# Where operands begin in a 512-byte line: other places for weights and for the low parts of inputs

## The chip, the cores and the metric

The kernel runs on one core of a Trainium2 chip. Its time is the device time in microseconds (us). Three runs of the kernel before gave 2886.08, 2892.32 and 2893.58 us; the median is 2892.32 us. The execution that the profile shows took 2885.26 us.

## The reference

Two networks of two layers each run one after the other on 256 tokens of width 1024 in 32-bit floats; the output of the first is the input of the second. The first network has a gated delta rule, a sliding-window attention and a squared-ReLU MLP; the second has two streams ("h", the tokens, and "c", a context of 256 tokens), attention, a short convolution and SwiGLU MLPs:

```
proj = rmsnorm(x, pre_mix_g) @ w_in                    # 1024 -> 7440
y_a = deltanet_branch(...) @ w_up_dn;  y_b = swa_sink_branch(...) @ w_up_sw
x = x + rmsnorm((sigmoid(gate_a) * y_a + sigmoid(gate_b) * y_b) @ w_o, post_mix_g)
x = x + rmsnorm(square(relu(rmsnorm(x, pre_mlp_g) @ w_ff1)) @ w_ff2, post_mlp_g)
# second network, twice per layer for each stream, around context_mix / latent_mix:
swiglu(u, wi, wo) = (silu(g) * up) @ wo,  with g, up = split(u @ wi)      # 1024 -> 2 x 2816 -> 1024
```

Nearly all arithmetic is in the products with the weights `w_in`, `w_ff1`, `w_ff2`, `ffn_wi`, `ffn_wo` and the output projections.

## The kernel before

**Products in three parts.** Every weight and every input of these products is kept as a high part and a low part, both of type fp32r (4 bytes). One product of 128 rows is three matmuls, in `mm3` (L264, L265, L266): high by high, high by low, low by high. In each, `lhsT` is the stationary operand (128 columns, loaded into the array by a weight load, "PEld") and `rhs` is the moving operand, read column by column.

**Two forms.** `lin_b` makes the weights stationary: tiles of 256 columns, called narrow here, of which each product takes 128; the moving operand is then 256 tokens of the input (`xTh`, `xTc`, `oT`). `lin_a`, `out_mm` and the first products of `layer1` make the inputs stationary (128 tokens) and let the weights move: tiles of 512, 432 or 384 columns, called wide. `by_tokens` is an exception: the tile is narrow, and its weights are the moving operand, 256 columns at a time, with the inputs stationary.

**The stages of a weight tile.** `wtile` (L231) issues a DMA of raw weights on SyncE's queue, ScalarE copies it to the high part (`hi`, L210) and VectorE subtracts for the low part (`lo`, L198). `hi` and `lo` have three buffers each.

**Places in a line.** A line here is 512 bytes (128 floats) of one partition's memory. All pools are padded (tiles tagged "line") so that tiles begin at a multiple of 512 bytes. `shifted` (L185) allocates each weight tile with 128 floats to spare and lets it begin further on: wide tiles at 0, narrow `hi` tiles at float 48 (byte 192), narrow `lo` tiles at float 96 (byte 384):

```
by = 0 if n > 256 else 48 if tag[:2] == "hi" else 96
flat = self.t(pool, [P, kt * n + 128], tag, F32R, bufs=bufs)
return flat[:, by:by + kt * n].rearrange("p (k n) -> p k n", n=n)
```

The inputs (`xTh`, `xTc`, made by `Norm.run`, L148), the MLPs' hidden rows (`hid`), `oT` and `mT` begin at byte 0, high and low parts alike. In a tile of 512, 384 or 256 columns every row of the tile is a multiple of 512 bytes long, so each begins at the place of its tile. A row of 432 columns is 1728 bytes, three lines and 192 bytes: four rows that follow each other begin at bytes 0, 192, 384 and 64.

**What sets the order.** The program's order is fixed when the kernel is built, by a scheduler that knows data dependences and priorities. `heads_by_columns` (L1277) prepares the queries of the second network's attention: `qs` and `qz` tiles of three buffers each; GpSimd clears `qz` (L1289) before ScalarE fills it.

Of the kernel before, what the change touches and what calls it, by code (L numbers as in the profile page):

```python
# [9 lines left out]
F32R = mybir.dt.float32r  # L10
# [7 lines left out]
P = 128  # L18
D = 1024
S = 256  # L20
KB = D // P
# [121 lines left out]
class Norm:  # L143


    def __init__(self, k, f, names=("h",)):
        self.k, self.f, self.names, self.x = k, f, names, {}

    def run(self, st, tb):
        if st.name not in self.names:  # L150
            return
        if st.name not in self.x:
            k = self.k
            self.x[st.name] = [k.t(k.xpool if st.name == "h" else k.xpool2, [P, KB, S], "xT" + st.name, F32R, bufs=2) for _ in range(2)]
        back = self.f(st, tb, *self.x[st.name])
        self.k.deferred.append([DEFER * 800, (st.name, tb), back])

# [6 lines left out]
class Kern:  # L164
    def __init__(self, tc, I, out, dbg=None):
        self.tc, self.nc, self.I, self.out, self.dbg = tc, tc.nc, I, out, dbg
        self.uid = 0
        self.flip = self.nraw = 0
        self.deferred = []
        self.credit = self.ada_rate = 0.0  # L170

# [13 lines left out]
    def shifted(self, pool, kt, n, tag, bufs):  # L185


        by = 0 if n > 256 else 48 if tag[:2] == "hi" else 96
        flat = self.t(pool, [P, kt * n + 128], tag, F32R, bufs=bufs)
        return flat[:, by:by + kt * n].rearrange("p (k n) -> p k n", n=n)  # L190

# [1086 lines left out]
    def heads_by_columns(self, ap, st, pj, qk, tb, kT):  # L1278


        nc = self.nc
        kh, kl, kb = kT
        qf = qk.rearrange("p h d -> p (h d)")
        s = slice(tb * P, (tb + 1) * P)
        q = None
        if st.full:
            q = self.t(ap, [P, 6, P], "qs", F32R, bufs=3), self.t(ap, [P, 2, 3, P], "qz", bufs=3)
            for d in range(2):
                nc.gpsimd.memset(q[1][64 - 64 * d:128 - 64 * d, d], 0.0)  # L1289
            for b in range(2):  # L1290
                ps = self.psum([P, 3, P])
                for j in range(3):
                    src = qf[:, j * P:(j + 1) * P] if b == 0 else pj[:, 384 + j * P:384 + (j + 1) * P]
                    nc.tensor.transpose(ps[:, j, :], src, self.ident)
                if b == 0:
                    self.stack_q(q[0], ps, 0.125)
                else:
                    for d in range(2):
                        r = slice(64 * d, 64 * d + 64)
                        self.act(q[1][r, d], ps[r], scale=0.125)  # L1300
        kd = self.t(self.work, [P, 4, 64], "w2", bufs=3)
        for d in range(2):
            nc.vector.tensor_copy(kd[:, d::2, :], qk[:, 6:8, :])
        kdf = kd.rearrange("p a d -> p (a d)")
        for j0, m in ((0, 2), (2, 3)):
            ps = self.psum([P, 3, P])
            for j in range(m):
                src = kdf[:, j * P:(j + 1) * P] if j0 == 0 else pj[:, 1024 + j * P:1024 + (j + 1) * P]
                nc.tensor.transpose(ps[:, j, :], src, self.ident)
            if j0 == 0:  # L1310
                self.split_psum(kh[:, :, s], kl[:, :, s], ps[:, :m, :])
            else:
                nc.vector.tensor_copy(kb[:, :, s], ps[:, :m, :])
        return q
# [193 lines left out]
```

## Time and profile before

| | |
|---|---|
| median of the three runs | 2892.32 us |
| the profiled execution | 2885.26 us |
| its span (first to last instruction) | 2883.5 us |
| TensorE busy | 2804.2 us (97%) |
| weight loads busy | 2608.6 us (90%) |
| VectorE busy | 2131.3 us (74%) |
| ScalarE busy | 1333.5 us (46%) |
| mean granted TensorE clock | 0.994 |

A matmul's record is longer than the time until the next one starts, since matmuls are pipelined: a record of 256 columns takes some 0.28 us, while the next one starts 0.12 us later. So the pace is read from the starts, as start of the last row minus start of the first, over the number of matmuls between them. Below, a triple is the three matmuls of one `mm3`.

### The profile page before, as it was taken

How to read it: one execution, taken by the hardware profiler on the slowest of the kernel's cores; microseconds unless marked ns; L12 is line 12 of the kernel's file. 1: busy time of each engine (PE TensorE's matmuls, PEld its weight loads, DVE VectorE, ACT ScalarE, POOL GpSimd, SP SyncE). 2: the span in 40 equal slices, each digit the busy share in tenths (PEclk: the TensorE clock that was granted, in tenths of full speed). 3: DMA queues.
4: the chain of work that ended last, by engine and by line, in shares of the span. 5: the costliest groups of instructions: out<-in, count | busy, mean ns of one | idle time of the engine just before them, and what ended most of it. 6: DMA issues, size and time to landing. Idle time of an engine off the chain costs nothing.

```text
span 2883.5 us, 51232 instructions
## 1 busy us (share of the span) xinstructions
PE 2804.2 (97%) x19840; PEld 2608.6 (90%) x19840; DVE 2131.3 (74%) x5043; ACT 1333.5 (46%) x2627; POOL 5.2 (0%) x16
## 2 busy tenths in 40 slices
PE   8999999999999999999999999999999999999998
PEld 7999988889989888999988988998989999888897
DVE  8888667897876778778698788877686554666764
ACT  6555454565545655332243556332353323446543
POOL 0000000000000000000000000000000000000000
PEclk9999999999999999999999999999999999999999
DMA  6632457655225566455435243555444442341564
GB/s 223 181 103 74 147 180 236 199 172 168 81 75 181 187 216 193 129 158 164 125 114 180 69 132 88 162 154 154 140 132 142 143 125 89 100 133 42 159 192 140
DMA packets 443908, 416.76 MB, mean 145 GB/s; under 512 B 18320, under 2 KB 383760, under 8 KB 443664
## 3 DMA queue, kind: packets, MB, share of 16 engines
q1 hardware_dynamic: 443664, 413.49, 47.2%
q8 instruction: 156, 2.56, 0.4%
q14 instruction: 88, 0.72, 0.1%
HBM read 412.37 MB, written 1.05 MB: 143 GB/s over the span
## 4 chain that ended last, share of the span: by engine, by line
PE 82%; DVE 9%; DMA 4%; ACT 4%; issue 2%; SPq 0%; DVEq 0%; ACTq 0%
PE mm L265 22%; PE mm L264 22%; PE mm L266 22%; PE sm L563 2%; DVE lo L198 2%; PE sm L515 2%; DVE acc L201 2%; PE sm L552 1%; DMA araw<-in_w_ada 1%; PE sm L805 1%; PE sm L800 1%; ACT hi L210 1%; PE sm L264 1%; PE sm L265 1%; PE sm L266 1%
## 5 line engine op out<-in xcount | busy, mean ns | idle before, releaser
L198 DVE TENSOR_TENSOR lo<-raw,hi 128x1024 fp32r<-128x1024 f32 (+2 forms) x628 | 750.4, 1206 | 334.6 <-ACT hi L210 333.5
L210 ACT ACTIVATE hi<-raw 128x1024 fp32r<-128x1024 f32 (+2 forms) x628 | 647.5, 1046 | 735.7 <-PE mm L265 314.0
L264 PE MATMUL mm<-xTh,hi 128*128 128x256 f32 x2336 | 655.7, 281 | 3.0 <-ACT xTh L210 3.0
L265 PE MATMUL mm<-xTh,hi 128*128 128x256 f32 x2336 | 652.7, 279 | 0.8 <-DVE xTh L201 0.8
L266 PE MATMUL mm<-xTh,lo 128*128 128x256 f32 x2336 | 649.2, 278 | 0.0
L265 PEld LDWEIGHTS mm<-xTh,hi 128*128 128x128 f32 x2336 | 442.2, 189 | 1.5 <-DVE xTh L201 1.2
L264 PEld LDWEIGHTS mm<-xTh,hi 128*128 128x128 f32 x2336 | 438.1, 188 | 3.7 <-ACT xTh L210 3.5
L266 PEld LDWEIGHTS mm<-xTh,lo 128*128 128x128 f32 x2336 | 438.4, 188 | 0.1
L201 DVE SCALAR_TENSOR_TENSOR acc<-araw,csil,acc 128x256 f32<-128x256 f32 x896 | 390.6, 479 | 64.3 <-DMA araw<-in_w_ada 61.6
L264 PE MATMUL mm<-hi,hid 128*128 128x512 f32 x872 | 340.4, 390 | 0.0
L266 PE MATMUL mm<-hi,hid 128*128 128x512 f32 x872 | 339.6, 389 | 0.0
L265 PE MATMUL mm<-lo,hid 128*128 128x512 f32 x872 | 339.5, 389 | 0.0
L264 PE MATMUL mm<-xTc,hi 128*128 128x256 f32 x1104 | 309.3, 280 | 0.0
L265 PE MATMUL mm<-xTc,hi 128*128 128x256 f32 x1104 | 307.1, 278 | 0.0
L266 PE MATMUL mm<-xTc,lo 128*128 128x256 f32 x1104 | 305.7, 277 | 0.0
L265 PEld LDWEIGHTS mm<-xTc,hi 128*128 128x128 f32 x1104 | 208.6, 189 | 0.4
L264 PEld LDWEIGHTS mm<-xTc,hi 128*128 128x128 f32 x1104 | 206.6, 187 | 0.4
L266 PEld LDWEIGHTS mm<-xTc,lo 128*128 128x128 f32 x1104 | 206.5, 187 | 0.1
L266 PEld LDWEIGHTS mm<-hi,hid 128*128 128x128 f32 x872 | 163.7, 188 | 34.2
L265 PEld LDWEIGHTS mm<-lo,hid 128*128 128x128 f32 x872 | 163.7, 188 | 33.4 <-DVE lo L198 0.2
L264 PEld LDWEIGHTS mm<-hi,hid 128*128 128x128 f32 x872 | 163.7, 188 | 33.1
L264 PE MATMUL mm<-hi,xTh 128*128 128x256 f32 (+3 forms) x512 | 178.0, 349 | 4.8 <-ACT xTh L1157 3.6
(323 smaller groups left out, 4647.8 us busy)
## 6 DMA issues: line engine op xcount, KB each, us to landing
raw<-in_ffn_wi SPq DMA_DIRECT2D x352, 256.0 KB, 3.7
araw<-in_w_ada SPq DMA_DIRECT2D x288, 256.0 KB, 2.9
raw<-in_w_ff SPq DMA_DIRECT2D x128, 512.0 KB, 4.1
raw<-in_w_in SPq DMA_DIRECT2D x116, 512.0 KB, 3.8
raw<-in_ffn_wo SPq DMA_DIRECT2D x88, 512.0 KB, 4.0
raw<-in_w_o SPq DMA_DIRECT2D x40, 512.0 KB, 3.4
raw<-in_w_in SPq DMA_DIRECT2D x24, 432.0 KB, 4.9
raw<-in_w_up_sw SPq DMA_DIRECT2D x16, 512.0 KB, 3.9
```

What stands on the lines that cost most here:

```text
L198: self.nc.vector.tensor_tensor(out=out, in0=a, in1=b, op=op)
L201: self.nc.vector.scalar_tensor_tensor(out=out, in0=a, scalar=s, in1=b, op0=op0, op1=op1)
L210: self.nc.scalar.activation(out, a, func, **kw)
L264: mm(ps, lhsT=ah, rhs=bh, start=first, stop=False)
L265: mm(ps, lhsT=ah, rhs=bl, start=False, stop=False)
L266: mm(ps, lhsT=al, rhs=bh, start=False, stop=last)
L515: nc.tensor.matmul(ps[:, h, o:o + n], lhsT=q, rhs=k, start=m == 0, stop=m == len(qk) - 1)
L552: nc.tensor.transpose(ps[:, b, :], sc[:, b // nb, (b % nb) * P:(b % nb + 1) * P], self.ident)
L563: nc.tensor.matmul(po[:, h, :], lhsT=pT[:, h * nb + kb, :], rhs=v, start=kb == 0, stop=kb == nb - 1)
L800: nc.tensor.matmul(ps[:, i, :], lhsT=LT[:, i, :], rhs=Dm[:, i, :], start=True, stop=True)
L805: nc.tensor.matmul(ps[:, i, :], lhsT=DT[:, i, :], rhs=M[:, i, :], start=True, stop=True)
```

## The change

Three things change, none of them a computation.

- Wide weight tiles begin at one of eight places (0, 64, ... 448 bytes) for `hi`, which goes on by one with every wide tile, and at one of eight for `lo`, which goes on by one with every eighth. Narrow tiles begin at byte 320 (`hi`) and 448 (`lo`).
- The inputs of `Norm` get 128 floats to spare. The high part begins at byte 0 still, the low part at one of the eight places, which goes on by one with every pair of tiles.
- `qz` has two buffers, not three.

```
-            self.x[st.name] = [k.t(..., [P, KB, S], "xT" + st.name, F32R, bufs=2) for _ in range(2)]
+            k.nx += 1
+            flat = [k.t(..., [P, KB * S + 128], "xT" + st.name, F32R, bufs=2) for _ in range(2)]
+            self.x[st.name] = [a[:, by:by + KB * S].rearrange("p (k t) -> p k t", t=S)
+                               for a, by in zip(flat, (0, 16 * (k.nx % 8)))]
...
-        by = 0 if n > 256 else 48 if tag[:2] == "hi" else 96
+        self.nw += n > 256 and tag[:2] == "hi"
+        by = (80 if tag[:2] == "hi" else 112) if n <= 256 else \
+             16 * (self.nw % 8 if tag[:2] == "hi" else self.nw // 8 % 8)
...
-            q = self.t(ap, [P, 6, P], "qs", F32R, bufs=3), self.t(ap, [P, 2, 3, P], "qz", bufs=3)
+            q = self.t(ap, [P, 6, P], "qs", F32R, bufs=3), self.t(ap, [P, 2, 3, P], "qz", bufs=2)
```

No instruction moves: on TensorE (17,550 rows), VectorE, ScalarE and SyncE the two programs have the same operations on the same tiles in the same order. Only waits differ, and most of these are around `qz`. GpSimd's part of the second network's attentions, before (the four `qz` tiles of the first layer, 17847 to 18368; a name in brackets is the engine that is waited for):

```order
L1289 MEMSET qz_17847 64x384 [waits DVE_49,PE_49]
L1289 MEMSET qz_17847 64x384
L1289 MEMSET qz_17903 64x384 x2
L1289 MEMSET qz_18306 64x384 [waits Activation_49]
L1289 MEMSET qz_18306 64x384
L1289 MEMSET qz_18368 64x384 [waits PE_49,Activation_49,Pool_49]
L1289 MEMSET qz_18368 64x384
```

and after:

```order
L1293 MEMSET qz_17847 64x384 [waits DVE_49,PE_49]
L1293 MEMSET qz_17847 64x384
L1293 MEMSET qz_17903 64x384 [waits PE_49]
L1293 MEMSET qz_17903 64x384
L1293 MEMSET qz_18306 64x384 [waits PE_49,Activation_49,Pool_49]
L1293 MEMSET qz_18306 64x384
L1293 MEMSET qz_18368 64x384 [waits PE_49,Activation_49,Pool_49]
L1293 MEMSET qz_18368 64x384
```

The third tile, 18306, now waits for the matmuls that read the first, and the fourth, 18368, for those that read the second.

## Rows read from the trace of the kernel before

**Rows 1.** The page, section 1: TensorE's busy time, share, instructions.

```profile
PE 2804.2 (97%) x19840; PEld 2608.6 (90%) x19840; DVE 2131.3 (74%) x5043; ACT 1333.5 (46%) x2627; POOL 5.2 (0%) x16
```

**Rows 2.** The page, section 4: the chain that ended last.

```profile
PE 82%; DVE 9%; DMA 4%; ACT 4%; issue 2%; SPq 0%; DVEq 0%; ACTq 0%
PE mm L265 22%; PE mm L264 22%; PE mm L266 22%; PE sm L563 2%; DVE lo L198 2%; PE sm L515 2%; DVE acc L201 2%; PE sm L552 1%; DMA araw<-in_w_ada 1%; PE sm L805 1%; PE sm L800 1%; ACT hi L210 1%; PE sm L264 1%; PE sm L265 1%; PE sm L266 1%
```

**Rows 3.** Groups by form: out<-in, shapes, count | busy us, mean ns | idle.

```profile
L264 PE MATMUL mm<-xTh,hi 128*128 128x256 f32 x2336 | 655.7, 281 | 3.0 <-ACT xTh L210 3.0
L265 PE MATMUL mm<-xTh,hi 128*128 128x256 f32 x2336 | 652.7, 279 | 0.8 <-DVE xTh L201 0.8
L266 PE MATMUL mm<-xTh,lo 128*128 128x256 f32 x2336 | 649.2, 278 | 0.0
...
L264 PE MATMUL mm<-hi,hid 128*128 128x512 f32 x872 | 340.4, 390 | 0.0
```

**Rows 4.** Timeline of TensorE, narrow products: start us, length us, instruction.

```profile
1257.67 0.36 PE L264 MATMUL mm<-xTh,hi 128*128 128x256 f32 x1
...
1329.75 0.27 PE L266 MATMUL mm<-xTh,lo 128*128 128x256 f32 x1
...
1400.38 0.28 PE L264 MATMUL mm<-xTc,hi 128*128 128x256 f32 x1
1400.50 0.28 PE L265 MATMUL mm<-xTc,hi 128*128 128x256 f32 x1
1400.62 0.28 PE L266 MATMUL mm<-xTc,lo 128*128 128x256 f32 x1
1400.73 0.28 PE L264 MATMUL mm<-xTc,hi 128*128 128x256 f32 x1
```

**Rows 5.** The same view, wide products of 512 columns (211 matmuls later).

```profile
2815.24 0.40 PE L264 MATMUL mm<-hi,hid 128*128 128x512 f32 x1
...
2863.07 0.48 PE L265 MATMUL mm<-lo,hid 128*128 128x512 f32 x1
```

**Rows 6.** The same view, wide products of 384 columns (95 matmuls later).

```profile
2560.67 0.33 PE L264 MATMUL mm<-hi,xTh 128*128 128x384 f32 x1
...
2577.16 0.34 PE L266 MATMUL mm<-hi,xTh 128*128 128x384 f32 x1
```

**Rows 7.** The same view, wide products of 432 columns (36 matmuls later).

```profile
35.72 0.36 PE L264 MATMUL mm<-hi,xTh 128*128 128x432 f32 x1
...
42.74 0.36 PE L264 MATMUL mm<-hi,xTh 128*128 128x432 f32 x1
```

**Rows 8.** The same view, products by tokens (27 matmuls later).

```profile
2693.15 0.28 PE L264 MATMUL mm<-hi,xTh 128*128 128x256 f32 x1
...
2696.36 0.28 PE L264 MATMUL mm<-hi,xTh 128*128 128x256 f32 x1
```

**Rows 9.** Timeline of TensorE; windows: stretch us, PE busy (count), PEclk, DMA share, GB/s.

```profile
667.61 0.41 PE L264 MATMUL mm<-oT,hi 128*128 128x256 f32 x1
...
669.32 0.33 PE L266 MATMUL mm<-oT,lo 128*128 128x256 f32 x1
...
667.50:669.40 1.90, 1.90 (x11) 0.50 0.02 6
1257.70:1329.70 72.00, 72.00 (x625) 1.00 0.46 140
```

**Rows 10.** Timelines of GpSimd, TensorE and ScalarE: the tiles `qz`.

```profile
1508.53 2.75 POOL L1289 MEMSET qz<- 64x384 f32 x6 [1508.08 <-PE mm L266]
1617.10 0.88 POOL L1289 MEMSET qz<- 64x384 f32 x2 [105.83 <-ACT sc L210]
...
1631.15 1.08 PE L515 MATMUL sm<-kb,qz 128*128 128x256 f32 x4
...
1638.42 0.98 ACT L210 ACTIVATE qz<-sm 64x384 f32<-64x384 f32 x2
1645.18 0.98 ACT L210 ACTIVATE qz<-sm 64x384 f32<-64x384 f32 x2
```

More of the change, by code (lines that the diff above doesn't have):

```diff
@@ L153, in run @@
             k = self.k
-            self.x[st.name] = [k.t(k.xpool if st.name == "h" else k.xpool2, [P, KB, S], "xT" + st.name, F32R, bufs=2) for _ in range(2)]
+            k.nx += 1
+            flat = [k.t(k.xpool if st.name == "h" else k.xpool2, [P, KB * S + 128], "xT" + st.name, F32R, bufs=2) for _ in range(2)]
+            self.x[st.name] = [a[:, by:by + KB * S].rearrange("p (k t) -> p k t", t=S) for a, by in zip(flat, (0, 16 * (k.nx % 8)))]
         back = self.f(st, tb, *self.x[st.name])
@@ L167, in __init__ @@
         self.uid = 0
-        self.flip = self.nraw = 0
+        self.flip = self.nraw = self.nw = self.nx = 0
         self.deferred = []
@@ L185, in shifted @@
     def shifted(self, pool, kt, n, tag, bufs):
-        by = 0 if n > 256 else 48 if tag[:2] == "hi" else 96
+        self.nw += n > 256 and tag[:2] == "hi"
+        by = (80 if tag[:2] == "hi" else 112) if n <= 256 else 16 * (self.nw % 8 if tag[:2] == "hi" else self.nw // 8 % 8)
         flat = self.t(pool, [P, kt * n + 128], tag, F32R, bufs=bufs)
```

## The prediction, made before the changed kernel had run

> **What bounds the kernel now.** I read the page from the top. TensorE is busy for 2804.2 of 2883.5 us [rows 1], and the chain that ended last lies on it for 82%: 22% on each line of `mm3` in tiles `mm` and 1% on each in tiles `sm`, together 69% or 1990 us [rows 2]. No instruction moves, so what is left to read is the pace of these products, and that is in the starts on the timeline, not in the lengths.
>
> Narrow products: 623 starts from 1257.67 to 1329.75 us are 115.7 ns apart in the mean [rows 4]. At a granted clock of 1.00 [rows 9], which is 2.4 GHz, 256 columns at one a cycle are 106.7 ns; each product takes 9.0 ns more. The three lines differ though they have one shape: L264 to L265 and L265 to L266 0.12 us, L266 to the next L264 0.11 us [rows 4], and mean records of 281, 279 and 278 ns [rows 3]. A triple is 347 ns, and with about 117 ns for each of the two longer steps some 113 ns are left for the short one. Wide products: 211 starts in 47.83 us are 226.7 ns apart [rows 5], 13.4 ns over the 213.3 ns of 512 columns; 384 columns take 173.6 ns [rows 6], 13.6 ns over 160.0.
>
> That surcharge is what the change can touch. It belongs to the full clock: at a granted 0.50 (1.2 GHz) 8 starts in 1.71 us are 213.8 ns apart, and 256 columns at 1.2 GHz are 213.3 [rows 9].
>
> **Counts.** Narrow stationary weights: 3,824 triples in four forms (2,336 of them `mm<-xTh,hi`). Wide: 1,224 triples of 512 columns in four forms (872 with `hid`) [rows 3], 96 of 384, 96 of 432. By tokens: 192. (The counts that no row shows are those of the loops.) The paces give 1327 + 833 + 50 + 56 + 68 = 2334 us for all of them; 1990 us of that are on the chain, so I let 0.85 of any change of pace through to the end. The rest would be taken up by waits for VectorE and DMAs that the products now hide.
>
> **Wide weights.** Before, the moving weights and the stationary inputs both begin at byte 0. Other places of moving weights are seen in one form only: rows of 432 columns begin at 0, 192, 384 and 64 in turn. Their pace is 7.02 us for 36, or 195.0 ns [rows 7], 15.0 ns over 180.0. So with places spread over the line the surcharge is 15.0 and not 13.4 to 13.6: 1.5 ns more. The change spreads the wide tiles evenly too: 3 x (1,224 + 96) = 3,960 matmuls x 1.5 ns = 5.9 us. The forms of 432 columns and by tokens stay as they are to me. Bounds: by tokens, where narrow weights move from bytes 192 and 384 over inputs at 0, 27 starts in 3.21 us are 118.9 ns apart [rows 8], a surcharge of 12.2, so 1.2 ns less than at 0 and -4.8 us; if the rows of 432 that begin at 0 have a surcharge of 13.4, the other three have (4 x 15.0 - 13.4) / 3 = 15.5, and were every wide tile off byte 0, that would be 2.1 ns or +8.3 us. I take the middle figure since it is the nearest row: a wide moving operand over an input at 0.
>
> **Low parts of the inputs.** In narrow products they move in L265, one matmul of three; 3,568 of these use tiles of `Norm` (the other 256 have `oT` or the delta rule's output). They too are spread over the line now. At the wide weights' +1.5 ns that is 5.4 us; at the 3.2 ns between by tokens and narrow [rows 4, 8] it would be 11.4 us; the lower end is 0. I take 5.4. In wide products they are the stationary operand of L266 in a quarter of the cases, for which I take 0.
>
> **Narrow weights.** They leave 192 and 384 for 320 and 448. Both are places off byte 0 before and after, and no row shows either new one, so I take 0. Bounds: all three lines at the shortest step, 113 ns, give 339 for 347, -8 ns x 3,824 = -31 us; all three at by tokens' 118.9 give 356.7, +9.7 x 3,824 = +37 us. These two ends are the two rivals with most weight.
>
> **`qz` with two buffers.** The third tile's two clears ran in the row of six at 1508.53 us and now wait as the fourth's do at 1617.10; the first tile's last reader is done by then. ScalarE fills the third tile at 1638.42, 21 us later. The fourth waits for the second tile's last reader, which starts at 1631.15 and is done by 1632.3; the fill is at 1645.18, 13 us later [rows 10]. Behind these clears GpSimd has nothing else. Cost 0; were the cover gone, two pairs of clears of 0.88 us each.
>
> **Sum.** 5.9 + 5.4 = 11.3 us of TensorE's time, x 0.85 = 9.6 us. The profiled execution took 2885.3 us (1.8 us of them around the span), which would become 2894.9. The median of the runs lies 7.1 us above that execution; I predict the median, 2892.3 + 9.6 = 2902 us.
>
> **Rivals.**
>
> *The new pair is the better one (faster).* For it: the short step after L266 shows that one and the same form can go at 113 ns, and L264 and L266 have the same moving operand, so that the weights' places, not the inputs', make the difference. Against: nothing says that 320 and 448 bring it to all three. Price: -31 + 5.9 = -25 us, x 0.85 = -21: 2871 us.
>
> *The distance counts (slower still).* If what decides is how far ahead in the line the weights begin, then the pair before had 192 (L264, L266's next) and 384, and the new one has 320 and 448 less the low part's place. By tokens the inputs are stationary at 0 and the weights move from 192: a distance of -192, which in a line of 512 is 320, and from 384, which is 128 [rows 8]. So L264 and L266 would take the pace of rows 8, and L265 passes all distances. Against it: rows 8 also differ by what moves. Price: (37 + 5.9) x 0.85 = +36: 2929 us. It decides from a narrow triple of 352 ns on, half way.
>
> *Places don't matter (no change).* The surcharge would belong to the fp32r stream as such, 9 ns with 256 columns and 13 to 15 with more. Against it stand the three lines of one shape with steps of 0.11 and 0.12 us [rows 4], and the 3.2 ns between rows 4 and rows 8, which have one shape too. Price: 0, 2892 us. This is where the Trainium skill would put it: "TensorE: Matmul & The Clock Gate", section "Step-by-step: what each phase is for", gives TensorE two independent read ports, one for the streaming operand and one for the weight load, and "SBUF — State Buffer", section "Specifications (TRN2)", has lines of 16 bytes, of which every place here is a multiple. By that rule nothing changes; the trace speaks against it, as the steps of rows 4 show.
>
> **Chances.** Forecast 0.31 (its own range 2893 to 2911), the better pair 0.28, the distance 0.24, no change 0.17. A measurement of this kernel can tell about 0.3%, 8.7 us, from no change. Of the forecast's cases about three in five lie over that, the rest within: slower 0.19 + 0.23 = 0.42. Same: 0.12 + 0.16 and 0.01 from each of the two outer cases = 0.30. Faster: 0.27 and 0.01 of the no-change case = 0.28. The range of 8 in 10 goes out to both outer rivals and a little beyond, 2866 to 2932 us, as the unknown places were bounded from -31 to +37 us.
>
> **What would show it.** In the changed kernel's timeline the narrow triple stays near 347 ns at `xTh` with a low part at byte 0 and gains some 1.5 ns elsewhere; 339 is the first rival, 356 the second. Wide products go from 226.7 to about 228 ns in the mean, with steps that differ from tile to tile as `hi` and `lo` change places; if all stay at 226.7 and the narrow ones at 115.7, places don't matter. The clears of the third and fourth `qz` come near 1617 and 1632 us with no idle time on ScalarE for them. I am wrong if the narrow products' pace moves by more than 2 ns either way, since that alone is worth 20 us.

## The result and the profile after

The changed kernel takes 2923.44 us (median of 4 runs, 2921.45 to 2925.73) against 2891.15 us (4 runs) of the kernel before on the same chip: a ratio of 1.0114, 95% interval 1.0097 to 1.0132. The forecast was 2902 us. The sign is right; the loss of 32 us is more than three times the 9.6 us predicted. The time lies in the stated range, 2866 to 2932 us, and outside the forecast's own, 2893 to 2911.

The profiled span grew by 36.8 us, from 2883.5 to 2920.3 us. The page of the kernel after, section 1 (busy us, share of the span, instructions) and section 4 (chain that ended last, by engine, then by line), in the form of [rows 1, 2]; `mm3` is now L268, L269 and L270:

```profile
PE 2845.8 (97%) x19840; PEld 2638.3 (90%) x19840; DVE 2132.4 (73%) x5043; ACT 1333.8 (46%) x2627; POOL 5.2 (0%) x16
...
PE 83%; DVE 8%; DMA 4%; ACT 3%; issue 1%; SPq 0%; DVEq 0%; ACTq 0%
PE mm L269 22%; PE mm L268 22%; PE mm L270 22%; PE sm L567 2%; DVE lo L202 2%; PE sm L519 2%; PE sm L556 1%; PE sm L809 1%; DVE acc L205 1%; DMA araw<-in_w_ada 1%; PE sm L804 1%; ACT hi L214 1%; PE sm L269 1%; PE sm L268 1%; PE sm L270 1%
```

TensorE is busy for 41.6 us more with the same 19,840 matmuls; VectorE and ScalarE stand where they stood, within 1.1 us. So the span did not grow by new waits: the same products go slower. The groups by form (count | busy us, mean ns of a record | idle), against [rows 3]:

```profile
L269 PE MATMUL mm<-xTh,hi 128*128 128x256 f32 x2336 | 663.9, 284 | 0.8 <-DVE xTh L205 0.8
L268 PE MATMUL mm<-xTh,hi 128*128 128x256 f32 x2336 | 658.8, 282 | 3.0 <-ACT xTh L214 3.0
L270 PE MATMUL mm<-xTh,lo 128*128 128x256 f32 x2336 | 660.7, 283 | 0.0
...
L268 PE MATMUL mm<-hi,hid 128*128 128x512 f32 x872 | 343.8, 394 | 0.0
```

The narrow records were 281, 279 and 278 ns long. It is not only the line that reads the low part (now L269, +5 ns) that got longer: L268 (+1) and L270 (+5) did too, though their moving operand still begins at byte 0. Wide records with `hid` went from 390 to 394 ns.

A group's mean hides that the pace changes from stage to stage. Three stretches of narrow products in the timeline of TensorE in the kernel after (start us, length us, instruction), the first and the last start of each; the low part of the input begins at byte 256, then 128, then 448:

```profile
2195.81 0.28 PE L268 MATMUL mm<-xTh,hi 128*128 128x256 f32 x1
...
2217.24 0.28 PE L268 MATMUL mm<-xTh,hi 128*128 128x256 f32 x1
```

```profile
480.29 0.28 PE L268 MATMUL sm<-xTh,hi 128*128 128x256 f32 x1
...
526.33 0.28 PE L268 MATMUL sm<-xTh,hi 128*128 128x256 f32 x1
```

```profile
2749.35 0.28 PE L268 MATMUL mm<-xTh,hi 128*128 128x256 f32 x1
2749.47 0.29 PE L269 MATMUL mm<-xTh,hi 128*128 128x256 f32 x1
2749.59 0.28 PE L270 MATMUL mm<-xTh,lo 128*128 128x256 f32 x1
2749.71 0.28 PE L268 MATMUL mm<-xTh,hi 128*128 128x256 f32 x1
...
2850.51 0.28 PE L268 MATMUL mm<-xTh,hi 128*128 128x256 f32 x1
```

These are 189 starts 113.4 ns apart, 381 starts 120.8 ns apart and 843 starts 120.0 ns apart; before, the pace was 115.7 ns [rows 4]. In the third all three steps are 0.12 us. The windows over the same three stretches and over two wide ones (stretch, busy us with count, granted clock, DMA share, GB/s) put the clock aside, as it is full everywhere. The DMAs' share differs little in the three narrow ones, 0.56 to 0.62 (e3 below has the third stretch's products at 113.4 ns with a share of 0.65); in the wide ones it differs more, and there the experiments have to show that it is the places:

```profile
480.30:526.30 46.00, 46.00 (x382) 1.00 0.62 192
2749.40:2850.50 101.10, 101.10 (x844) 1.00 0.62 183
2195.90:2217.20 21.30, 21.30 (x190) 1.00 0.56 176
...
1373.90:1384.10 10.20, 10.20 (x46) 1.00 0.55 156
2256.95:2267.40 10.45, 10.45 (x46) 1.00 0.76 215
```

All places of the low part, each by one long stretch of the same timeline that is free of waits (byte 0 by `oT`, the others by tiles of `Norm`):

| low part at byte | starts | from, to (us) | ns apart |
|---|---|---|---|
| 0 | 90 | 115.54, 125.74 | 113.3 |
| 256 | 189 | 2195.81, 2217.24 | 113.4 |
| 64 | 189 | 305.27, 327.53 | 117.8 |
| 320 | 92 | 1157.39, 1168.23 | 117.8 |
| 128 | 381 | 480.29, 526.33 | 120.8 |
| 384 | 141 | 1168.59, 1185.61 | 120.7 |
| 192 | 189 | 873.27, 895.95 | 120.0 |
| 448 | 843 | 2749.35, 2850.51 | 120.0 |

Two things are to be seen. Places 256 bytes apart agree, within 0.1 ns. And with the low part at 0 or 256 the new weights' places give 113.3 ns on all three lines: the new pair is better than the old one, and the low parts' places take back more than it gives.

Wide products of 512 columns with `hid`, in the kernel after's timeline: weights at bytes 256 and 0 (high, low), which modulo 256 is 0 and 0, then at 448 and 256, which is 192 and 0:

```profile
1373.88 0.39 PE L268 MATMUL mm<-hi,hid 128*128 128x512 f32 x1
...
1384.12 0.39 PE L268 MATMUL mm<-hi,hid 128*128 128x512 f32 x1
```

```profile
2256.90 0.39 PE L268 MATMUL mm<-hi,hid 128*128 128x512 f32 x1
...
2267.44 0.40 PE L268 MATMUL mm<-hi,hid 128*128 128x512 f32 x1
```

45 starts each, 227.6 and 234.2 ns apart; before, all went at 226.7 [rows 5].

**The account.** For every triple I took the time from its first start to the next triple's first start, left out those with a wait in them, and sorted the rest by the places at which the program puts their operands. Mean ns of a triple:

| products | triples | before | after | difference, us of TensorE |
|---|---|---|---|---|
| narrow, stationary weights | 3,824 | 347.5 | 354.7 | +27.5 |
| wide, 512 columns | 1,224 | 683.1 | 695.3 | +14.9 |
| wide, 384 and 432 columns | 96 + 96 | 520.6, 587.6 | 524.3, 590.9 | +0.7 |
| by tokens | 192 | 356.4 | 352 | -0.8 |

Together +42.3 us, where the page's busy time grew by 41.6 us and the span by 36.8 us (0.87 of 42.3). These are the two profiled executions; the medians of the runs are 32.3 us apart (0.76). The narrow row is the sum of two that the experiments take apart below: -26 us by the new pair and +54 us by the low parts.

**`qz`.** GpSimd's clears of the third and the fourth tile, the last readers of the first and of the second tile on TensorE, and ScalarE's fills in the kernel after (as [rows 10]):

```profile
1631.76 0.88 POOL L1293 MEMSET qz<- 64x384 f32 x2 [108.50 <-ACT sc L214]
1647.05 0.88 POOL L1293 MEMSET qz<- 64x384 f32 x2 [14.40 <-ACT sc L214]
...
1630.53 1.08 PE L519 MATMUL sm<-kb,qz 128*128 128x256 f32 x4
...
1645.82 1.08 PE L519 MATMUL sm<-kb,qz 128*128 128x256 f32 x4
...
1653.10 0.97 ACT L214 ACTIVATE qz<-sm 64x384 f32<-64x384 f32 x2
1659.85 0.98 ACT L214 ACTIVATE qz<-sm 64x384 f32<-64x384 f32 x2
```

Each clear starts right behind its readers, which end at 1631.6 and 1646.9 us. The clears start 21.3 and 12.8 us ahead of their fills, and the fills' rows show no idle time ahead of them. Predicted were 21 and 13 us.

### The profile page after: what moved, and what is told of

Same layout as the page of the kernel before. It is cut to its first block, busy times and chain, and to the rows that moved or that the text cites. A ratio compares the mean times of both kernels' runs of the same rounds, so it can differ in the third digit from the quotient of the medians.

```text
span 2920.3 us, 51235 instructions
## 1 busy us (share of the span) xinstructions
PE 2845.8 (97%) x19840; PEld 2638.3 (90%) x19840; DVE 2132.4 (73%) x5043; ACT 1333.8 (46%) x2627; POOL 5.2 (0%) x16
## 4 chain that ended last, share of the span: by engine, by line
PE 83%; DVE 8%; DMA 4%; ACT 3%; issue 1%; SPq 0%; DVEq 0%; ACTq 0%
PE mm L269 22%; PE mm L268 22%; PE mm L270 22%; PE sm L567 2%; DVE lo L202 2%; PE sm L519 2%; PE sm L556 1%; PE sm L809 1%; DVE acc L205 1%; DMA araw<-in_w_ada 1%; PE sm L804 1%; ACT hi L214 1%; PE sm L269 1%; PE sm L268 1%; PE sm L270 1%
## 5 line engine op out<-in xcount | busy, mean ns | idle before, releaser
L269 PE MATMUL mm<-xTh,hi 128*128 128x256 f32 x2336 | 663.9, 284 | 0.8 <-DVE xTh L205 0.8
L268 PE MATMUL mm<-xTh,hi 128*128 128x256 f32 x2336 | 658.8, 282 | 3.0 <-ACT xTh L214 3.0
L270 PE MATMUL mm<-xTh,lo 128*128 128x256 f32 x2336 | 660.7, 283 | 0.0
L268 PEld LDWEIGHTS mm<-xTh,hi 128*128 128x128 f32 x2336 | 443.3, 190 | 3.7 <-ACT xTh L214 3.5
L269 PEld LDWEIGHTS mm<-xTh,hi 128*128 128x128 f32 x2336 | 442.3, 189 | 1.5 <-DVE xTh L205 1.2
L270 PEld LDWEIGHTS mm<-xTh,lo 128*128 128x128 f32 x2336 | 443.0, 190 | 0.1
L268 PE MATMUL mm<-hi,hid 128*128 128x512 f32 x872 | 343.8, 394 | 0.0
L270 PE MATMUL mm<-hi,hid 128*128 128x512 f32 x872 | 342.9, 393 | 0.0
L269 PE MATMUL mm<-lo,hid 128*128 128x512 f32 x872 | 342.7, 393 | 0.0
L269 PE MATMUL mm<-xTc,hi 128*128 128x256 f32 x1104 | 312.5, 283 | 0.0
L270 PE MATMUL mm<-xTc,lo 128*128 128x256 f32 x1104 | 311.7, 282 | 0.0
L268 PE MATMUL mm<-xTc,hi 128*128 128x256 f32 x1104 | 311.5, 282 | 0.0
L268 PEld LDWEIGHTS mm<-xTc,hi 128*128 128x128 f32 x1104 | 209.4, 190 | 0.4
L270 PEld LDWEIGHTS mm<-xTc,lo 128*128 128x128 f32 x1104 | 209.6, 190 | 0.1
L269 PEld LDWEIGHTS mm<-xTc,hi 128*128 128x128 f32 x1104 | 208.5, 189 | 0.5
L270 PEld LDWEIGHTS mm<-hi,hid 128*128 128x128 f32 x872 | 163.8, 188 | 37.7
L269 PEld LDWEIGHTS mm<-lo,hid 128*128 128x128 f32 x872 | 163.8, 188 | 36.8
L268 PEld LDWEIGHTS mm<-hi,hid 128*128 128x128 f32 x872 | 163.7, 188 | 36.7
L268 PE MATMUL mm<-hi,xTh 128*128 128x256 f32 (+3 forms) x512 | 180.0, 353 | 4.7 <-ACT xTh L1161 3.3
```

Of the source, the lines that this page charges most:

```text
L268: mm(ps, lhsT=ah, rhs=bh, start=first, stop=False)
L269: mm(ps, lhsT=ah, rhs=bl, start=False, stop=False)
L270: mm(ps, lhsT=al, rhs=bh, start=False, stop=last)
```

## The experiments

Theory A: the new pair is the better one and its gain is hidden by the low parts' places, which slow the whole triple. Theory B, the prediction's rival "the distance counts": the pair itself is the worse one, with L264 and L266 at the pace of by tokens. All but the last two were timed several times, together with the kernel before; these two ran once, for tables of places.

**e1_low_at_0** (edit of the kernel after): low parts of the inputs back at 0.

```
-  ... for a, by in zip(flat, (0, 16 * (k.nx % 8)))]
+  ... for a, by in zip(flat, (0, 0))]
```

> The changed kernel with the low parts of the inputs back at byte 0 (narrow weights at 320 and 448, wide weights spread). Theory A, the low parts' places cost: in the changed kernel a narrow triple takes 340 ns where the low part lies at 0 or 256 and 354 to 365 ns elsewhere, 354.7 in the mean; with all at 0 it is 340 ns everywhere, 14.7 x 3,824 = 56 us less, x 0.85 = 48: about 2876 us (2868 to 2884). Theory B, the distance (the new pair itself is to blame): the triple stays above 352 ns and the time above 2912 us.

2879.37 us, ratio to the kernel before 0.9969 (0.9958 to 0.9981); narrow triples 340.7 ns, wide ones of 512 columns 695.1. A holds, B falls: one edit of the moving operand of a single line takes some 42 us off the changed kernel, by the two ratios (1.0114 and 0.9969), and makes it faster than the one before.

**e2_wide_at_0** (edit of the kernel after): wide weights back at 0.

```
-  by = (80 if tag[:2] == "hi" else 112) if n <= 256 else 16 * (self.nw % 8 if ...)
+  by = 0 if n > 256 else 80 if tag[:2] == "hi" else 112
```

> The changed kernel with wide weights back at byte 0. Theory A: the 512-column triple goes from 695.3 back to 683.1 ns, 12.2 x 1,224 = 15 us, x 0.85 = 13: about 2910 us (2905 to 2915). Theory B has no price for the wide weights: within 5 us of 2923.

2915.94 us, just over the 2905 to 2915 expected, ratio 1.0085 (1.0065 to 1.0104), narrow 354.7, wide 684.1. The pace came back as expected, 11.2 ns x 1,224 = 13.7 us of TensorE's time; of the end only some 8 us did, by the two ratios, 1.0114 and 1.0085. With both intervals that is some 1 to 16 us, so the 0.85 of the prediction is neither confirmed nor refuted here.

**e3_pair_alone** (edit of the kernel before): only the narrow weights' new places.

```
-  by = 0 if n > 256 else 48 if tag[:2] == "hi" else 96
+  by = 0 if n > 256 else 80 if tag[:2] == "hi" else 112
```

> The kernel before with narrow weights at 320 and 448, nothing else. Theory A: narrow triple 347.5 to 340.5 ns, -7 x 3,824 = -27 us, x 0.85 = -23: about 2868 us (2860 to 2876), faster than before. Theory B: triple 356 ns, about 2922 us, slower.

2867.2 us, ratio 0.9928 (0.9914 to 0.9941): faster than both kernels, and the lowest median of all; those of e6 and e7 lie within its interval. Narrow triples 340.7 ns, wide ones 683.1 as before. Its groups by form, the three narrow lines:

```profile
L265 PE MATMUL mm<-xTh,hi 128*128 128x256 f32 x2336 | 652.2, 279 | 0.8 <-DVE xTh L201 0.8
L264 PE MATMUL mm<-xTh,hi 128*128 128x256 f32 x2336 | 651.4, 279 | 3.0 <-ACT xTh L210 3.0
L266 PE MATMUL mm<-xTh,lo 128*128 128x256 f32 x2336 | 651.0, 279 | 0.0
```

and the stretch that answers to the changed kernel's 843 starts, in the timeline and as a window:

```profile
2703.78 0.28 PE L264 MATMUL mm<-xTh,hi 128*128 128x256 f32 x1
...
2799.34 0.28 PE L264 MATMUL mm<-xTh,hi 128*128 128x256 f32 x1
...
2703.80:2799.30 95.50, 95.50 (x845) 1.00 0.65 193
```

95.56 us for 843, 113.4 ns, at a granted clock of 1.00 and a DMA share of 0.65 (the window below the rows; 0.62 in the changed kernel); the same products took 101.16 us with the low part at 448. The three lines' records are now equal, where [rows 3] had 281, 279 and 278. B would have had 357 ns a triple.

**e4_qz2** (edit of the kernel before): `qz` with two buffers, nothing else.

```
-  ... self.t(ap, [P, 2, 3, P], "qz", bufs=3)
+  ... self.t(ap, [P, 2, 3, P], "qz", bufs=2)
```

> The kernel before with two qz buffers, nothing else. Theory A and the prediction: the clears go to about 1617 and 1632 us, 21 and 13 us ahead of their use, time within 0.2% of before. A rival that the lost buffer costs something: over 3 us slower, with idle time on ScalarE before the fills of qz.

2889.24 us, ratio 1.0002 (0.9992 to 1.0011). No cost.

This run also shows that places do not settle the pace alone. The program puts the operands of the following products at the same addresses in the kernel before (first two rows) and in e4 (last two):

```profile
1062.42 0.28 PE L264 MATMUL sm<-xTh,hi 128*128 128x256 f32 x1
...
1089.81 0.28 PE L264 MATMUL sm<-xTh,hi 128*128 128x256 f32 x1
```

```profile
1062.39 0.28 PE L264 MATMUL sm<-xTh,hi 128*128 128x256 f32 x1
...
1089.60 0.28 PE L264 MATMUL sm<-xTh,hi 128*128 128x256 f32 x1
```

These are 237 starts 115.6 ns apart and 231 starts 117.8 ns apart, 347 and 353 ns a triple, at a granted clock of 1.00 and a DMA share of 0.54 and 0.53. From 979 to 991 us it is the kernel before that goes at 353 and e4 at 347. Some 5 to 7% of each kernel's narrow stretches without waits go at 353, so the means over all narrow triples agree within 0.3 ns. What selects the pace is open.

**e5_low_at_128, e6_low_at_256, e7_all_on_64** (edits of the kernel after, each with wide weights at 0): is it a matter of the low part alone, has it a period, and do places count or only distances?

```
-  ... for a, by in zip(flat, (0, 16 * (k.nx % 8)))]
+  ... for a, by in zip(flat, (0, 32))]        # e5: low part at byte 128
+  ... for a, by in zip(flat, (0, 64))]        # e6: low part at byte 256
+  ... for a, by in zip(flat, (16, 16))]       # e7: both parts at byte 64
-  by = (80 if tag[:2] == "hi" else 112) if n <= 256 else ...
+  by = 0 if n > 256 else 80 if tag[:2] == "hi" else 112      # e5, e6
+  by = 0 if n > 256 else 96 if tag[:2] == "hi" else 128      # e7: narrow at 384 and 512
```

> Narrow weights at 320 and 448, wide at 0, the low parts of all inputs of Norm at byte 128. Theory A: their narrow triples take 365 ns as in the changed kernel at that place, 25 ns over the pair alone: 25 x 3,568 = 89 us, x 0.85 = 76 over the pair alone's 2867: about 2943 us (2930 to 2955). Rival, a low part's place matters only where it changes from stage to stage or with the spread of the wide weights: about 2867.

2934.17 us, ratio 1.0155 (1.0141 to 1.0169). The same 843 starts in its timeline:

```profile
2759.89 0.28 PE L268 MATMUL mm<-xTh,hi 128*128 128x256 f32 x1
...
2861.79 0.28 PE L268 MATMUL mm<-xTh,hi 128*128 128x256 f32 x1
```

120.9 ns apart, the worst place; over all narrow triples 361.1 ns.

> The same with the low parts at byte 256. Theory A with a period of 256 bytes: triple 340 ns, as with the pair alone, about 2867 us (within 0.3%). Rival, the line of 512 bytes counts: the triple lies between 350 and 365 ns, 2895 to 2943 us.

2871.01 us, ratio 0.9938 (0.9925 to 0.9952), narrow 340.6 ns: a low part at 256 is as good as one at 0. Between e5 and e6 lie 20.5 ns x 3,824 = 78 us of TensorE's time and 63 us of the end, 0.81; between e1 and e3 15 us (the wide weights alone) and 12.2 us, 0.82. So the prediction's 0.85 was about right, though a little high by both.

> Everything of the narrow products goes 64 bytes on: high and low parts of Norm's inputs at 64, narrow weights at 384 and 512; wide weights at 0. If only the places relative to each other count: narrow triples of Norm's inputs 340 ns, about 2867 us (up to 2875, as 288 wide triples of 512 columns and 96 of 384 now have inputs at 64). If the moving operand's own place counts (only byte 0 or 256 is cheap): triples of 350 ns and more, 2895 us or more.

2870.44 us, ratio 0.9937 (0.9923 to 0.995). Two stretches of its timeline, first 90 starts with `oT`, which stays at 0 under weights at 384 and 512, then the 843 starts with everything moved by 64:

```profile
115.62 0.28 PE L268 MATMUL mm<-oT,hi 128*128 128x256 f32 x1
...
126.28 0.29 PE L268 MATMUL mm<-oT,hi 128*128 128x256 f32 x1
```

```profile
2704.95 0.29 PE L268 MATMUL mm<-xTh,hi 128*128 128x256 f32 x1
...
2800.53 0.28 PE L268 MATMUL mm<-xTh,hi 128*128 128x256 f32 x1
```

118.4 and 113.4 ns. Moved together the set keeps its pace, moved apart it loses it: what counts is the places against each other, as far as this one shift shows. Wide triples of 512 columns whose inputs alone moved to 64 went from 680 to some 700 ns (median).

**e9_hid_pair** (edit of the kernel before): the pair of e3, and the same arrangement in the wide products with `hid` and `mT`, whose stationary high part now begins at 320 and low part at 448, over weights that move from 0.

```
-  hid[key] = [self.t(hp, [P, S], "hid", F32R, bufs=hid_bufs) for _ in range(2)]
+  hid[key] = self.pair(hp, [P, S], "hid", hid_bufs // 2)     # tiles with spacers of 80 and 32 floats; likewise mT
```

> The pair alone, and also the stationary inputs of wide products that are nothing else (hid, mT) at 320 and 448, wide weights at 0. If wide products follow the same table as narrow ones (moving at 0, stationary at 320, 320, 448: a surcharge of 6.7 ns in place of 13.4): 512 columns in 220 ns with hid and mT, 936 triples x 3 x 6.7 = 19 us, x 0.85 = 16 under the pair alone: about 2851 us (2845 to 2858). Rival, the surcharge of longer moving operands doesn't depend on where the weight load reads: 226.7 ns, 2867 us.

2877.76 us, ratio 0.9964 (0.995 to 0.9977). Both expected times were missed, 2851 and 2867 us. 189 starts with `hid` in the timeline of this kernel, and of e3 where `hid` is at 0:

```profile
993.10 0.39 PE L278 MATMUL mm<-hi,hidh 128*128 128x512 f32 x1
...
1036.91 0.39 PE L278 MATMUL mm<-hi,hidh 128*128 128x512 f32 x1
```

```profile
994.43 0.40 PE L264 MATMUL mm<-hi,hid 128*128 128x512 f32 x1
...
1037.29 0.39 PE L264 MATMUL mm<-hi,hid 128*128 128x512 f32 x1
```

231.8 against 226.8 ns. The stationary operand's place does count in wide products, but the arrangement that is best for 256 columns is no good for 512: 936 triples with `hid` and `mT` x 13 ns (medians 693 and 680) x 0.85 = 10 us, the distance to e3.

**e8_probe_pairs** (edit of the kernel before, one run): the narrow weights pass through all 64 pairs of places, with inputs at 0.

```
-  by = 0 if n > 256 else 48 if tag[:2] == "hi" else 96
+  by = 0 if n > 256 else 16 * (self.nw % 8 if tag[:2] == "hi" else self.nw // 8 % 8)
```

> The kernel before with narrow weights at each of the 64 pairs of places in turn, inputs and wide weights at 0: a table, not a version. Theory A with a period of 256 bytes: the four pairs that equal (320, 448) up to 256 bytes take 340 ns a triple, the four that equal (192, 384) take 347, and the 64 fall into 16 groups of four whose medians agree within 2 ns. If (320, 448) is the best of them, no group lies under 339 ns; a group near 335 ns would be 5 x 3,824 x 0.85 = 16 us better. Rival, the line of 512 bytes counts: the groups of four spread by over 5 ns.

2912.29 us, beside 2885.05 of the kernel before. Its narrow triples by places modulo 256 (ns a triple, by groups of 16 triples without a wait):

| high at \ low at | 0 | 64 | 128 | 192 |
|---|---|---|---|---|
| 0 | 360 | 353 | 357 | 353 |
| 64 | 353 | 353, once 347 and 341 | 354 to 356 | **340** |
| 128 | 355 | 353 or 357 | 356 or 360 | 350 or 360 |
| 192 | 353 | 357, once 340 | **347** | 353 |

Expected was that places which are alike modulo 256 agree within 2 ns. In eleven of the sixteen cells they do; in five one and the same pair goes at two paces or more. It is not the line of 512 bytes that parts them: the groups from 997.7 and from 2285.9 us, with all operands at the same addresses (weights at 448 and 64), take 340 and 357 ns. So the table holds as in e4, up to the pace that a stretch takes.

Two stretches of its timeline, high and low at (64, 192), then at (0, 0), each of 93 starts:

```profile
1901.99 0.28 PE L265 MATMUL mm<-xTc,hi 128*128 128x256 f32 x1
...
1912.53 0.28 PE L265 MATMUL mm<-xTh,hi 128*128 128x256 f32 x1
```

```profile
1310.23 0.28 PE L265 MATMUL mm<-xTc,hi 128*128 128x256 f32 x1
...
1321.39 0.28 PE L265 MATMUL mm<-xTh,hi 128*128 128x256 f32 x1
```

113.3 and 120.0 ns. The pair of the change, 320 and 448, is (64, 192), the only one of the sixteen that goes at 340 ns (at most 342) in every such group; the pair before, 192 and 384, is (192, 128), the second best.

**e10_probe_wide** (edit of the kernel before, one run): the pair of e3; weights of 512 columns at all 16 pairs of 0, 64, 128 and 192, and the low parts of `hid` and `mT` at 64, 128 or 192 by stage.

```
+  by = ... 16 * (self.nw % 4 if tag[:2] == "hi" else self.nw // 4 % 4) if n == 512 else 0
+  q = 16 * (1 + sum(a.startswith("ff") for a in self.order) % 3)     # low part of hid and mT
```

> The pair alone, with 512-column weights at each of 16 pairs (0 to 192 bytes, high and low) and the low parts of hid and mT at 64, 128 or 192 by stage, their high parts at 0: a table, not a version. With the changed kernel's 16 pairs over inputs at 0 this is every arrangement modulo 256 bytes and modulo a common shift. The changed kernel's least is 680 ns a triple, with all at 0. If wide products have a pair as good as the narrow ones' (6.7 ns over the columns), some group takes 660 ns; if all at 0 is the least of all 64 arrangements, none lies under 679 ns.

2883.16 us, beside 2893.43. No arrangement goes below the 680 ns of a triple with all at 0; the next, with weights at 64 and 128 and the low input at 128, takes some 685 in the mean, the worst some 707 (median). Of these arrangements the wide products had been at the best.

## Why the prediction came out right in sign and too small

- *What bounds the kernel.* Held. The whole difference is the pace of the same matmuls, and 0.76 (medians) to 0.87 (profiled executions) of it reached the end where 0.85 had been taken; e5 against e6, the largest step, gives 0.81.
- *Low parts of the inputs: "At the wide weights' +1.5 ns that is 5.4 us", bounds 0 and 11.4 us.* **This step failed.** It measured +54 us: 14.0 ns a triple (354.7 against 340.7 in e1 and e3) x 3,824. Two errors lie in it. It charged one matmul of three, the one that reads the low part; in fact the lines before and after it slow down as well. With the low part at 128 the three steps are 117, 122 and 121 ns (medians), and 113 each with it at 0. And it took the price of another form, wide moving weights, whose table of places is not that of 256 columns (e9).
- *Narrow weights: "no row shows either new one, so I take 0".* Measured -26 us: -6.8 ns x 3,824. The first rival's mechanism, all three lines at the short step of [rows 4], was right with nearly its whole price, -31 us, and e3 shows it alone.
- *Wide weights: +1.5 ns a matmul, 5.9 us, bounds -4.8 and +8.3.* Right in sign, too small: 12.2 ns a triple or 4.1 ns a matmul, 15 us. The rows of 432 columns [rows 7] were no measure. Weights and inputs at 0, as in [rows 5], are the best of 64 arrangements modulo 256 (e10), so every move off them costs, 7.5 ns a matmul in the slower stretch shown above (234.2 for 226.7). The zero for low parts as stationary operands was wrong too: in e5 135 starts of 512 columns with `xTh` and `xTc` as stationary operands (2570.87 to 2602.08 us) went at 231.2 ns, those with `hid` at 226.9.
- *`qz`: 0.* Right, with the cover as read (21 and 13 us), and e4 shows it alone.
- *"Places don't matter"* fell: paces from 113.3 to 120.8 ns for one and the same form at full clock, with places that are all multiples of 64 bytes. The Trainium skill, "TensorE: Matmul & The Clock Gate", section "Step-by-step: what each phase is for", has the streaming operand and the weight load read through two independent ports, so that a load takes no read bandwidth from the running matmul. The trace of e9 does not bear this out in full: the stationary operand's place by itself slows wide products by 5.0 ns a matmul. The load is not longer for it: its records last 188 ns in the stretches of e9 and of e3 alike, and end 41 and 36 ns (mean) before the next matmul starts.
- *"The distance counts"* named the time nearest to the measured one, 2929 us, and its own test, a triple above 352 ns, was met with 354.7. Its mechanism fell all the same: L264 and L266 go at 113 ns with the new pair (e3), and the loss left with the low parts (e1). One number had two possible causes, and only undoing each part told them apart. What is right in it is that distances count (e7), but those of the whole set, modulo 256.
- *"I am wrong if the narrow products' pace moves by more than 2 ns either way."* It moved by 2.4 ns (347.5 to 354.7 a triple), the net of -2.3 by the pair and +4.7 by the low parts. So by its own sign the prediction was wrong on how the time comes about.

The errors had opposite signs, and the right sign of the sum is luck: with the pair's -26 us and the forecast's own two terms it would have been a gain. The time fell into the stated range because that range reaches to both outer rivals. The terms as measured, -26 + 54 + 15 = 43, x 0.85 = 37 us, are the 36.8 us between the profiled spans; the medians are 32.3 us apart.

Open is why: what in the chip has a period of 256 bytes, why a place slows the lines beside its own, why 512 columns have another table, and why one arrangement can go at two paces (e4, e8). No run here looks inside that, and the tables are measured, not derived.

## What to carry to other kernels

Where a pace lies a few per cent above one column a cycle and lines of one shape have different steps, the starting places of operands are worth a table: one kernel that passes through all pairs, sorted by place in its trace, takes one run and names the candidates. Look at several stretches of each, as some arrangements go at two paces. Change one operand's places at a time, as a gain (26 us here) can be buried under a loss from the next edit (54 us); and don't price one form by another's rows, since 256 and 512 columns like different arrangements.

## What was not expected of the hardware

- The pace of a product depends on where its operands begin relative to each other modulo 256 bytes: 113.3 to 120.9 ns for 256 columns, 226.8 to 234.2 for 512, at a granted clock of 1.00. Moved by 256 bytes (e6) or all together by 64 (e7) they keep their pace.
- It belongs to the sequence, not to one matmul: moving the moving operand of one line of three from 0 to 128 adds 4, 9 and 8 ns to the three steps.
- The stationary operand's place counts in wide products as well: 680 to 693 ns a triple (e9).
- One arrangement can go at two paces, each held for whole stretches: 115.6 and 117.8 ns with the same addresses and the same clock (kernel before and e4), 340 and 357 ns a triple in e8.
